# Last transposition of a head pair moved into the output sums' bank and ahead of the Newton product; the recurrence's results kept in one bank on diagonal quarters of the matrix unit

## The chip, the cores and the metric

The kernel runs on one core of one Trainium2 chip. A core has five engines that run their own instruction queues and wait for each other by semaphores: TensorE (PE in the profile, matrix products; its weight loads are PEld), VectorE (DVE), ScalarE (ACT), GpSimd (POOL) and SyncE (SP, which here issues the transfers). PE writes its results into PSUM, a small memory of eight banks of 2 KB a partition, and DVE and ACT read them from there; everything else on the core lies in SBUF.

The metric is the device time of one execution in microseconds (us). Before the change it is 1246.86 us, the median of three runs (1245.12, 1246.86 and 1247.34). A difference under 0.2% (about 2.5 us) is about what a measurement of this kernel can't tell from no change.

## The reference

Two layers over 256 positions of width 2048. Each layer normalises, makes one input projection, and feeds two groups of heads; their results are gated, joined, projected and added to the input. The part that the change touches is the group of 16 recurrent heads of width 64, each scanned in both directions (cut to what matters):

```python
for l in range(DEPTH):
    h = rms_norm(x, norm_g[l])
    proj = jnp.einsum('btd,dc->btc', h, w_in[l])
    ...
    y_rw = rwkv7_branch(r, k, v, xw, xa, w0[l], decay_up[l], a0[l], iclr_up[l], ...)
    ...
    y_at = window_attention(qh, kh, vh, sink[l]).astype(x.dtype)
    mix = jnp.concatenate([y_rw * jax.nn.silu(g_rw), y_at * jax.nn.silu(g_at)], axis=-1)
    x = x + jnp.einsum('btc,cd->btd', mix, w_out[l])

def wkv_scan(r, decay, k, v, kk, a, reverse):
    def step(S, inp):
        r_t, w_t, k_t, v_t, kk_t, a_t = inp
        s_kk = jnp.einsum('bhvk,bhk->bhv', S, kk_t)
        S = (S * w_t[:, :, None, :]
             - s_kk[..., None] * (a_t * kk_t)[:, :, None, :]
             + v_t[..., None] * k_t[:, :, None, :])
        return S, jnp.einsum('bhvk,bhk->bhv', S, r_t)
    ...

# in rwkv7_branch, behind both directions' scans:
mu = jnp.mean(y, -1, keepdims=True)
var = jnp.mean(jnp.square(y - mu), -1, keepdims=True)
yn = (y - mu) * lax.rsqrt(var + LNX_EPS)
yn = yn * lnx_g... + lnx_b...
out = yn + bonus * vh
```

## The kernel before

**Chunks and pairs.** The 256 positions are cut into four chunks of 64, and the heads are worked two at a time: eight pairs a layer, one head in partitions 0 to 63 and one in 64 to 127 (`half[0]`, `half[1]`). A product of 64x64 uses one quarter of PE's array, named by the half of the partitions it reads and the half it writes. Within a chunk the recurrence is a triangular system; its inverse is built by doubling blocks (levels of 2 up to 32) and by one Newton step.

**The work of one pair** is three generators, cut at `yield` into steps:
- `scan_p`: decays, keys and gates of the pair.
- `scan_i`: the masked products GE (L718 on PE, L724 on DVE, one of each for each direction), AB and AL, their fp16 parts (L733 on ACT, L764 on DVE), the transposes `pt` (L741, L749) that ACT reads as `bt` (L754) and, in four copies, as first values of the state `suv` (L759); then the inverse, level by level, from products `pq` and `pd` (L803 at the first level; L813, L819, L821 at the others) that DVE puts into two matrices `tv` and `tt` under masks (L806, L808, L809, L822, L823); last the Newton product `pf` (L829 to L834) and, in two steps of their own, FN (L836) and `pn` (L840), from which DVE makes `vf` in one operation over 128 partitions x 512 elements (L842).
- `scan_b`: the recurrence over the four chunks. For each: `pr` (L866), copied as `rh` (L869, at the first chunk two copies of L872), `pu` (L885), copied to the state `suv` (L890), the next state `pS` (L895, L897), and the output sums `py` (L877, L902). Behind the last chunk: the sums of squares (L913 to L915), the normalised output `ysq` (L917), its transposition on PE `pz` (L922), which ACT scales to `t` (L924), to which DVE adds `bv` (L925) and which `mix_split` gates and splits into MH and ML (L614 to L616), the operand of the output projection.

**PSUM.** `ps_main` holds two banks of the projections' sums `pm`. `ps_c` holds one bank `pcc` (the states of a pair) and one bank `py` (the output sums, in its first half; the second half holds one `pr` of the first chunk). `ps_w` holds two buffers of two banks, which all the other products (pza, pk, pbn, pg, pt, pq, pd, pf, pn, pu, pyt and the attention's) take in turn, in the order in which the program asks for them: each waits for the readers of the product that had the buffer two requests earlier. `wpair` takes such a buffer, `wbank` takes one and uses its first half.

**Windows and slots.** The big projections run beside these steps. Their weights are converted in tiles of 128x512 into a high part on ACT (L215, `hi`) and a low part on DVE (L216, `lo`), and a step of a projection is three products over 256 columns (L273, L274, L275). A window has 14 slots (numbered 0 to 13); in each slot the program first issues the scans' steps, then four or five projection steps, 64 in a window. Window w works on four pairs at once: the last step of pair w-4's `scan_b`, the two last steps of pair w-3's `scan_i` (`pf` in slot 0, `pn` in slot 1) and its `scan_b` (a step in each slot from 1 to 13), pair w-2's `scan_i` up to its last level (slots 0 to 13), and pair w-1's `scan_p`. The tables `STAGE_P`, `STAGE_I`, `STAGE_B` say in which slots. The last step of pair w-4 (`pz` and what follows) stands in slot 3. Each layer has four windows that are alike, with all four pairs at work (called steady below; 42.8 us each). The one ahead of them, called the first window below, has no pair w-4 yet; thinner ones stand ahead of it, and behind the steady ones come windows in which the attention's operations take the place of `scan_p`. Of these the tenth of a layer (382 to 425 us in the first layer, called the late window below) still has `scan_i`, `scan_b` and the last step of a pair in it.

PE's order is the program's order; the order of ACT and DVE is made by a scheduler that places instructions by priority, with that of `scan_b` raised by 95 (`PRIO_B`).

Of the kernel before, what the change touches and what calls it, by code (L numbers as in the profile page):

```python
# [9 lines left out]
F32 = mybir.dt.float32  # L10
# [5 lines left out]
AF = mybir.ActivationFunctionType  # L16
ALU = mybir.AluOpType
# [4 lines left out]
T = 256  # L22
# [13 lines left out]
P_NG, P_MU0, P_MU1, P_KK, P_KA, P_RK, P_LG, P_LB, P_A0 = 0, 16, 42, 68, 76, 84, 92, 100, 108  # L36
# [7 lines left out]
SLOTS = 14  # L44
STAGE_P = [4, 6, 7, 8, 9, 10, 11, 13]
STAGE_I = (list(range(SLOTS)), [0, 1])
STAGE_B = (list(range(1, 14)), [3])
ATT = [
    [4, 11],
    [1, 3, 6, 8, 11, 13],  # L50
# [78 lines left out]
def hybrid_trunk_kernel(ctx, tc, xT, wi, wv, wo, par, fing, dup, iup, sink, pos, cst, out):  # L129
    nc = tc.nc  # L130
    V, A, G, PE, SY = nc.vector, nc.scalar, nc.gpsimd, nc.tensor, nc.sync

    def pool(name, bufs, **kw):
        return ctx.enter_context(tc.tile_pool(name=name, bufs=bufs, **kw))
# [471 lines left out]
    def layer(l):  # L606
        L = layers[l]
        prm = lambda o, j: PR[:, l, o + j : o + j + 1]
# [99 lines left out]
        def scan_i(p, t):  # L708
            VV, BK, MV = t["v"], t["BK"], t["MV"]
            flat = lambda x: x.rearrange("p d c j -> p (d c) j")  # L710
            GE = st("ge", [2, 2, NC, 2, 64], bufs=2)
            GE = [GE[:, h] for h in range(2)]
            GEd = lambda d: pick(GE[0], every, d * NC * 128, [2 * NC * 128, 2], [128, NC], [1, 128])
            for d in range(2):
                pg = wpair("pg")
                for c in range(NC):
                    for h in range(2):
# [4 lines left out]
                            start=True, stop=True,  # L722
# [32 lines left out]
            SUV = st("suv", [2, NC, 2, 64], bufs=2)  # L755
# [26 lines left out]
            TT = st("tt", [2, NC, 64], F16)  # L782
# [43 lines left out]
            o = lambda d, c, h: pf[half[h ^ d], d, c * 64 : (c + 1) * 64]  # L826
# [11 lines left out]
            pn = wbank("pn")  # L838
            for d, c, h in dch:
                PE.matmul(pn[half[h ^ d], d * T + c * 64 : d * T + (c + 1) * 64], hx(FN, d, c, h), hx(TT, d, c, h), start=True, stop=True)  # L840
            VF = st("vf", [2, NC * 64])
            V.scalar_tensor_tensor(  # L842
                VF.rearrange("p d x -> p (d x)"), TT.rearrange("p d c j -> p (d c j)"), 2.0, pn, op0=ALU.mult, op1=ALU.add
            )
            t["VF"] = VF
            yield

        def scan_b(p, t):
            GE, MV, BT, SUV, PC, bv = (t[n] for n in ("GE", "MV", "BT", "SUV", "PC", "bv"))


            pc = ps_c.tile([128, 512], F32, tag="c", name="pcc")
            pS = pc[:, 0:128].rearrange("p (d j) -> p d j", d=2)
            pyt = ps_c.tile([128, 512], F32, tag="y", name="py")
            py = pyt[:, 0:256].rearrange("p (c j) -> p c j", j=64)
            for i in range(NC):
                ci = [order[d][i] for d in range(2)]

                here = lambda h, i=i: pick(SUV, half[h], i * 128 + h * 64, [NC * 128 + (NC - 1 - 2 * i) * 128, 2], [1, 64])

                pr = [pc[:, 128:192], pc[:, 192:256] if i else pyt[:, 256:320]]
                for d in range(2):
                    for h in range(2):

                        r = half[1 - h] if i == 0 else every
                        PE.matmul(pr[d][half[h ^ d]], GE[h][r, d, ci[d], 0, :], SUV[r, d, ci[d], h, :], start=True, stop=True)  # L866
                RH = st("rh", [2, 64], bufs=2)
                if i:
                    A.activation(RH, pc[:, 128:256].rearrange("p (d j) -> p d j", d=2), AF.Copy)  # L869
                else:  # L870
                    for d in range(2):
                        A.activation(RH[:, d, :], pr[d], AF.Copy)  # L872
                yield
                if i > 0:
                    for d in range(2):
                        for h in range(2):
                            PE.matmul(  # L877
                                py[half[h], ci[d], :], MV[half[h], d, ci[d], 1, :], SUV[half[h], d, ci[d], h, :],
                                start=False, stop=False, skip_group_check=True,
                            )  # L880
                pu = wpair("pu")
                for d in range(2):
                    for h in range(2):
                        x = half[h ^ d]
                        PE.matmul(pu[half[h], d, 0:64], t["VF"][x, d, cs(ci[d])], RH[x, d, :], start=True, stop=True)  # L885
                if 0 < i < NC - 1:
                    for h in range(2):
                        PE.matmul(pS[half[h]], ident[half[h], half[h]], here(h), start=True, stop=False, skip_group_check=True)  # L888
                for h in range(2):
                    A.activation(here(h), pu[half[h], :, 0:64], AF.Copy)  # L890
                yield
                if i < NC - 1:
                    for d in range(2):
                        for h in range(2):
                            PE.matmul(pS[half[h], d, :], BT[:, h, d, i, :], SUV[:, d, ci[d], h, :], start=(i == 0), stop=True, skip_group_check=True)  # L895
                    for h in range(2):
                        V.tensor_tensor(  # L897
                            here(h, i + 1), pS[half[h]], pick(PC, half[h], i, [2 * NC - 1 - 2 * i, 2], [0, 64]), op=ALU.mult
                        )
                for d in range(2):  # L900
                    for h in range(2):
                        PE.matmul(  # L902
                            py[half[h], ci[d], :], GE[h][:, d, ci[d], 1, :], SUV[:, d, ci[d], h, :],
                            start=(i == 0 and d == 0), stop=(i >= NC // 2), skip_group_check=True,
                        )
                if i < NC - 1:
                    yield


            ysq = st("ysq", [NC, 64])  # L910
            yv = st("yv", [NC])
            for c in range(NC):
                A.activation(ysq[:, c], py[:, c], AF.Square, accum_out=yv[:, c : c + 1])  # L913
            V.tensor_scalar(yv, yv, 1.0 / 64, LNX_EPS, op0=ALU.mult, op1=ALU.add)
            G.tensor_tensor(yv, yv, mhalf, op=ALU.pow)  # L915
            yield
            V.tensor_tensor(ysq, py, yv.unsqueeze(2).to_broadcast([128, NC, 64]), op=ALU.mult)  # L917
            yield
            pz = wbank("pyt")
            for c in range(NC):  # L920
                for h in range(2):
                    PE.matmul(pz[half[h], cs(c)], ysq[half[h], c, :], ident[half[h], half[h]], start=True, stop=True)  # L922
            Zt = st("t1", [T], bufs=3)
            A.activation(Zt, pz[:, 0:T], AF.Identity, scale=prm(P_LG, p), bias=prm(P_LB, p))  # L924
            V.tensor_tensor(Zt, Zt, bv, op=ALU.add)  # L925
            mix_split(p, Zt, t["gr"])
            yield
# [3 lines left out]
        def scans(w):  # L931

            gens = []
            for lag, scan, at in ((4, scan_b, STAGE_B[1]), (3, scan_i, STAGE_I[1]), (3, scan_b, STAGE_B[0]), (2, scan_i, STAGE_I[0]), (1, scan_p, STAGE_P)):
                p = w - lag
                if 0 <= p < NP:
                    if (scan, p) not in chains:
                        chains[scan, p] = scan(p, L.ts[p])
                    gens.append((chains[scan, p], at))
            return gens  # L940
# [119 lines left out]
    for a, b in ((0, 2), (2, 4), (4, 8), (8, 12), (12, 16)):  # L1060
        x = X2[:, a:b, :]
# [83 lines left out]
```

## Time and profile before

| | before |
|---|---|
| device time, median of 3 runs | 1246.86 us |
| device time of the profiled execution | 1247.3 us |
| span of the profiled execution | 1245.5 us |
| mean granted TensorE clock | 0.987 |
| busy share of the span: PE, DVE, ACT, POOL | 95%, 75%, 59%, 2% |
| chain that ended last: PE, DVE, issue, ACT, DMA | 48%, 18%, 16%, 11%, 4% |
| of that chain on L273, L274 and L275 (the projections' products) | 13%, 11%, 11% |

The span runs from the first to the last instruction; the device time is 1.8 us longer. Busy shares are averages over the span, and the chain is followed back from the last instruction to what released each one. In the timeline a row gives the start, the time to the end of the last of the group, the engine, the line, the operation, the tile written and the tiles read, the shape and the count, and in brackets how long the engine stood idle before it and who released it. A product of fp32 numbers counts as two matrix instructions in these rows. The ends of matrix products are modelled, so differences of starts are the better measure on PE.

### The profile page before, as it was taken

The page shows a single profiled execution, that of the slowest core. Times are in us where ns is not written, and L with a number is a line of the kernel's source. Part 1 is how long each engine was busy: PE and PEld are TensorE (multiplying, and loading weights), DVE is VectorE, ACT ScalarE, POOL GpSimd, SP SyncE. Part 2 cuts the span into 40 slices and gives each one's busy share as a digit, 9 for nine tenths or more (in the row PEclk, how much of TensorE's full clock was granted, in tenths as well). Part 3 has the DMA queues.
Part 4 walks back from the last instruction along what each step waited for, and adds up shares of the span by engine and source line. Part 5 has one row for each costly group of instructions (what it writes and reads, how often), then busy time and mean ns, then how long its engine had stood idle before and what let it go on. Part 6 is the DMA issues. An engine that isn't in the chain of part 4 may idle for free.

```text
span 1245.5 us, 38032 instructions
## 1 busy us (share of the span) xinstructions
PE 1184.3 (95%) x16140; PEld 1092.3 (88%) x16140; DVE 937.5 (75%) x2082; ACT 739.9 (59%) x1838; POOL 19.0 (2%) x23
## 2 busy tenths in 40 slices
PE   6989999999998999999999999999999989999996
PEld 6978888888887989989998888888888888899996
DVE  6878878887976678856666888878887766786654
ACT  6646665766565466645555656665766555675553
POOL 0000000000000000000000000000000000000000
PEclk9999999999999999999999999999999999999998
DMA  7443233322322434466554433233223324435653
GB/s 246 156 143 122 88 116 109 105 93 94 134 77 93 133 109 142 140 204 224 210 182 143 143 110 119 93 111 109 104 93 100 112 99 131 140 130 174 212 190 119
DMA packets 60410, 166.70 MB, mean 134 GB/s; under 512 B 7728, under 2 KB 22736, under 8 KB 60240
## 3 DMA queue, kind: packets, MB, share of 16 engines
q1 hardware_dynamic: 60240, 164.27, 38.5%
q8 instruction: 126, 2.06, 0.7%
q14 instruction: 44, 0.36, 0.1%
HBM read 157.43 MB, written 4.19 MB: 130 GB/s over the span
## 4 chain that ended last, share of the span: by engine, by line
PE 48%; DVE 18%; issue 16%; ACT 11%; DMA 4%; SPq 1%; POOL 0%; DVEq 0%; POOLq 0%; ACTq 0%
PE pm L273 13%; PE pm L275 11%; PE pm L274 11%; DVE lo L216 3%; DMA g<-dup 3%; PE pg L718 2%; DVE kd L665 2%; ACT hi L215 2%; DVE ge L724 2%; ACT AB L733 2%; ACT suv L759 2%; DVE lw L659 2%; ACT ge L771 1%; DMA rrot<-u 1%; ACT bt L754 1%
## 5 line engine op out<-in xcount | busy, mean ns | idle before, releaser
L273 PE MATMUL pm<-XH,hi 128*128 128x256 f32 x1664 | 498.1, 299 | 14.5 <-ACT XH L178 6.1
L275 PE MATMUL pm<-XH,lo 128*128 128x256 f32 x1664 | 471.4, 283 | 11.2 <-DVE lo L216 11.2
L274 PE MATMUL pm<-XL,hi 128*128 128x256 f32 x1664 | 470.6, 283 | 0.1
L215 ACT ACTIVATE hi<-raw 128x512 fp32r<-128x512 f32 x560 | 329.6, 625 | 212.1 <-PE pm L274 170.0
L216 DVE TENSOR_TENSOR lo<-raw,hi 128x512 fp32r<-128x512 f32 x560 | 369.0, 687 | 84.0 <-ACT hi L215 76.7
L273 PEld LDWEIGHTS pm<-XH,hi 128*128 128x128 f32 x1664 | 316.5, 190 | 40.2 <-issue 13.0
L275 PEld LDWEIGHTS pm<-XH,lo 128*128 128x128 f32 x1664 | 316.8, 190 | 14.6 <-DVE lo L216 14.4
L274 PEld LDWEIGHTS pm<-XL,hi 128*128 128x128 f32 x1664 | 317.3, 191 | 0.8 <-DVE XL L179 0.8
L273 PE MATMUL pm<-MH,hi 128*128 128x256 f32 x512 | 145.5, 284 | 2.3 <-ACT hi L215 2.3
L275 PE MATMUL pm<-MH,lo 128*128 128x256 f32 x512 | 145.2, 284 | 0.1
L274 PE MATMUL pm<-ML,hi 128*128 128x256 f32 x512 | 145.0, 283 | 0.0
L273 PEld LDWEIGHTS pm<-MH,hi 128*128 128x128 f32 x512 | 97.9, 191 | 3.2 <-ACT hi L215 2.5
L275 PEld LDWEIGHTS pm<-MH,lo 128*128 128x128 f32 x512 | 97.8, 191 | 0.4 <-DVE lo L216 0.4
L274 PEld LDWEIGHTS pm<-ML,hi 128*128 128x128 f32 x512 | 98.0, 191 | 0.0
L890 ACT ACTIVATE suv<-pu 64x128 f32<-64x128 f32 x128 | 34.5, 270 | 24.8 <-PE pcc L888 13.6
L724 DVE TENSOR_TENSOR ge<-pg,C 128x1024 f32<-128x1024 f32 x32 | 39.1, 1221 | 3.5 <-PE pg L718 3.5
L970 ACT ACTIVATE mv<-mv,mx 128x257 f32<-128x257 f32 x64 | 31.9, 504 | 15.9 <-DVE mx L967 15.9
L733 ACT ACTIVATE AB<-ge 64x512 f16<-64x512 f32 x32 | 20.2, 630 | 34.3 <-DVE ge L724 33.9
L718 PE MATMUL pg<-mv,bk 64*128 64x128 f32 x512 | 37.2, 285 | 0.0
L822 DVE CAST_PREDICATED tv<-LV,pd 128x256 f16<-128x256 uint8 x80 | 34.0, 426 | 4.1 <-PE pd L821 3.7
L815 ACT ACTIVATE QF<-pq 128x256 f16<-128x256 f32 x80 | 30.8, 385 | 6.8 <-PE pq L813 5.5
L823 DVE CAST_PREDICATED tt<-LV,pd 128x256 f16<-128x256 uint8 x80 | 34.0, 425 | 0.0
(241 smaller groups left out, 1833.7 us busy)
## 6 DMA issues: line engine op xcount, KB each, us to landing
raw<-wi SPq DMA_DIRECT2D x207, 512.0 KB, 3.8
raw<-wo SPq DMA_DIRECT2D x64, 512.0 KB, 3.8
raw<-wv SPq DMA_DIRECT2D x8, 512.0 KB, 3.6
rrot<-u SPq DMA_DIRECT2D x80, 32.0 KB, 2.3
vg<-xT SPq DMA_DIRECT2D x16, 128.0 KB, 3.6
xd<-vg SPq DMA_DIRECT2D x16, 128.0 KB, 3.6
vg<-xd SPq DMA_DIRECT2D x16, 128.0 KB, 3.5
g<-dup SPq DMA_DIRECT2D x16, 97.0 KB
```

The source lines that it names most:

```text
L215: A.activation(hi[:, q], raw[:, q], AF.Copy)
L216: V.tensor_tensor(lo[:, q], raw[:, q], hi[:, q].bitcast(F32), op=ALU.subtract)
L273: PE.matmul(pm, wh, rh[:, kk, :], start=(kk == 0), stop=False)
L274: PE.matmul(pm, wh, rl[:, kk, :], start=False, stop=False)
L275: PE.matmul(pm, wl, rh[:, kk, :], start=False, stop=(kk == 15))
L718: PE.matmul(pg[:, h, c * 128 : (c + 1) * 128], BK[half[h], d, c, 1 - h : 3 - h, :].rearrange("p s j -> p (s j)"), MV[half[h], d, c].rearra ...
L724: V.tensor_tensor(GEd(d), pg.rearrange("p h (c x) -> p h c x", c=NC), gm[d].unsqueeze(1).unsqueeze(1).to_broadcast([128, 2, NC, 128]), op= ...
L733: A.activation(flat(AB[half[h]]), GE[h][half[h]].rearrange("p d c s j -> p (d c) s j")[:, :, 0, :], AF.Copy)
L822: V.copy_predicated(t_sub(TC), t_mask, flat4(pd[:, :, 0:128]))
L823: V.copy_predicated(v_sub(TT), v_mask, flat4(pd[:, 0, 128:384].rearrange("p (d x) -> p d x", d=2)))
L890: A.activation(here(h), pu[half[h], :, 0:64], AF.Copy)
L970: A.activation(Sc[:, h, q, 0:257], Sc[:, h, q, 0:257], AF.Exp, scale=0.125, bias=mx[:, q : q + 1], accum_out=den[:, q : q + 1])
```

## The change

It has three parts.

First, `pz` no longer takes a buffer of `ps_w`: it is written into the second half of the pair's own bank of output sums (`pyt[:, T : 2 * T]`), which the first chunk's `pr` no longer uses. And its step is issued in slot 1 instead of slot 3 (`STAGE_B`), where it stands ahead of pair w-3's `pn`. With it move the ACT copy to `t`, the DVE addition of `bv`, and the three operations of `mix_split`. No transfer belongs to that step.

Second, `pr`, `pu` and `pS` of a chunk lie in one tile of the bank of states, asked for anew for each chunk, `pc` of [128, 3, 2, 64]. So `pu` takes no buffer of `ps_w` either. `pr` of the first chunk and `pu` are computed with each head reading and writing its own half of the partitions (two quarters of PE's array, on the diagonal) where before the second direction crossed over (four quarters). `rh` of the first chunk is one ACT copy and not two.

Third, for that the second direction of `vf` must lie in the other half of the partitions, so `vf` is written by three DVE operations (one of 128 partitions x 256, two of 64 partitions x 256 that cross over) in place of one of 128 x 512.

```diff
-STAGE_B = (list(range(1, 14)), [3])
+STAGE_B = (list(range(1, 14)), [1])
...
             VF = st("vf", [2, NC * 64])
-            V.scalar_tensor_tensor(
-                VF.rearrange("p d x -> p (d x)"), TT.rearrange("p d c j -> p (d c j)"), 2.0, pn, op0=ALU.mult, op1=ALU.add
-            )
+            for o, i, d in ((every, every, 0), (half[0], half[1], 1), (half[1], half[0], 1)):
+                V.scalar_tensor_tensor(
+                    VF[o, d], TT[i, d].rearrange("p c j -> p (c j)"), 2.0, pn[i, d * T : (d + 1) * T], op0=ALU.mult, op1=ALU.add
+                )
...
-            pc = ps_c.tile([128, 512], F32, tag="c", name="pcc")
-            pS = pc[:, 0:128].rearrange("p (d j) -> p d j", d=2)
...
-                pr = [pc[:, 128:192], pc[:, 192:256] if i else pyt[:, 256:320]]
+                pc = ps_c.tile([128, 3, 2, 64], F32, tag="c", name="pcc")
+                pS = pc[:, 2]
...
-                        PE.matmul(pr[d][half[h ^ d]], GE[h][r, d, ci[d], 0, :], SUV[r, d, ci[d], h, :], start=True, stop=True)
+                        PE.matmul(pc[half[h], 0, d, :], GE[h][r, d, ci[d], 0, :], SUV[r, d, ci[d], h, :], start=True, stop=True)
                 RH = st("rh", [2, 64], bufs=2)
-                if i:
-                    A.activation(RH, pc[:, 128:256].rearrange("p (d j) -> p d j", d=2), AF.Copy)
-                else:
-                    for d in range(2):
-                        A.activation(RH[:, d, :], pr[d], AF.Copy)
+                A.activation(RH, pc[:, 0], AF.Copy)
...
-                pu = wpair("pu")
                 for d in range(2):
                     for h in range(2):
-                        x = half[h ^ d]
-                        PE.matmul(pu[half[h], d, 0:64], t["VF"][x, d, cs(ci[d])], RH[x, d, :], start=True, stop=True)
+                        PE.matmul(pc[half[h], 1, d, :], t["VF"][half[h], d, cs(ci[d])], RH[half[h], d, :], start=True, stop=True)
...
-            pz = wbank("pyt")
+            pz = pyt[:, T : 2 * T]
```

What moves, at three places of a steady window. The first is PE's order in slot 1 (pn is the Newton product's second half, q and tt its operands; L915 is the changed kernel's line of pz):

```order
 L274 MATMUL pm<-XL,hi 128x256
 L275 MATMUL pm<-XH,lo 128x256
+L915 MATMUL py<-C,ysq 64x64 x8
 L840 LDWEIGHTS q_2653
 L840 MATMUL pn<-tt,q_2653 64x64
```

And in slot 3 of the same window (L895 and L902 are the next state and the output sums before, L888 and L895 the same two in the changed kernel):

```order
 L274 MATMUL pm<-XL,hi 128x256
 L275 MATMUL pm<-XH,lo 128x256
-L922 MATMUL pyt<-C,ysq 64x64 x8
-L895 MATMUL pcc<-suv,bt 64x64 x4
-L902 MATMUL py<-suv,ge 64x64 x4
+L888 MATMUL pcc<-suv,bt 64x64 x4
+L895 MATMUL py<-suv,ge 64x64 x4
 L803 LDWEIGHTS AB
 L803 MATMUL pq<-tv,AB 64x32
```

The eight transposing products go from slot 3, where they stood between the projection and L803, to slot 1 ahead of pn.

The second place is DVE's order in slots 1 and 2, first before the change (ge is GE, tv and tt the inverse's two matrices, set to the unit matrix by L784):

```order
L784 COPY tv<-EYE 128x512
L724 TENSOR_TENSOR ge<-pg,C 128x2x512
L842 SCALAR_TENSOR_TENSOR vf<-tt,pn 128x512
L784 COPY tt<-EYE 128x512
L724 TENSOR_TENSOR ge<-pg,C 128x2x512
L764 TENSOR_TENSOR AL<-ge,AB 64x512 x2
```

and behind the change (L843 is vf, L918 the addition of bv):

```order
L784 COPY tv<-EYE 128x512
L724 TENSOR_TENSOR ge<-pg,C 128x2x512
L843 SCALAR_TENSOR_TENSOR vf<-tt,pn 128x256
L918 TENSOR_TENSOR t_5355<-t_5355,bv 128x256
L843 SCALAR_TENSOR_TENSOR vf<-tt,pn 64x256
L614 SCALAR_TENSOR_TENSOR mf<-t_5355,vg 128x256
L843 SCALAR_TENSOR_TENSOR vf<-tt,pn 64x256
L784 COPY tt<-EYE 128x512
L616 TENSOR_TENSOR ML<-mf,MH 128x256
L724 TENSOR_TENSOR ge<-pg,C 128x2x512
```

Between the two operations that make GE there stood one operation of vf and the setting of tt; now there stand three of vf, the setting, and the three operations that follow pz.

The third place is DVE's order in slots 4 to 6, before (kr, iu and du belong to the projection's results, lw and mv to scan_p, L822 and L823 put pd into tv and tt):

```order
L402 SCALAR_TENSOR_TENSOR kr<-u,PR,kr 128x255
L442 TENSOR_TENSOR iu<-g,iuh 96x256
L656 TENSOR_SCALAR lw<-lw 128x512
L442 TENSOR_TENSOR du<-g,duh 97x256
L659 SCALAR_TENSOR_TENSOR lw<-MSK,lw 128x256 x2
L822 COPY_PREDICATED tv<-LV,pd 128x2x64x2
L823 COPY_PREDICATED tt<-LV,pd 128x2x64x2
L673 SCALAR_TENSOR_TENSOR mv<-pp,kkr 128x4x63
L674 SCALAR_TENSOR_TENSOR mv<-pp,kkr 128x4x63
```

and behind the change:

```order
L442 TENSOR_TENSOR du<-g,duh 97x256
L442 TENSOR_TENSOR iu<-g,iuh 96x256
L656 TENSOR_SCALAR lw<-lw 128x512
L659 SCALAR_TENSOR_TENSOR lw<-MSK,lw 128x256 x2
L673 SCALAR_TENSOR_TENSOR mv<-pp,kkr 128x4x63
L674 SCALAR_TENSOR_TENSOR mv<-pp,kkr 128x4x63
L822 COPY_PREDICATED tv<-LV,pd 128x2x64x2
L823 COPY_PREDICATED tt<-LV,pd 128x2x64x2
```

L673 and L674 now stand ahead of L822 and L823. This second order is the one that the first window of each layer has already before the change. The orders of SP and POOL are the same in both kernels, and requests for buffers of `ps_w` fall from 26 to 19 in a steady window.

More of the change, by code (lines that the diff above doesn't have):

```diff
@@ L889, in scan_b @@
                 for h in range(2):
-                    A.activation(here(h), pu[half[h], :, 0:64], AF.Copy)
+                    A.activation(here(h), pc[half[h], 1], AF.Copy)
                 yield
@@ L923, in scan_b @@
             Zt = st("t1", [T], bufs=3)
-            A.activation(Zt, pz[:, 0:T], AF.Identity, scale=prm(P_LG, p), bias=prm(P_LB, p))
+            A.activation(Zt, pz, AF.Identity, scale=prm(P_LG, p), bias=prm(P_LB, p))
             V.tensor_tensor(Zt, Zt, bv, op=ALU.add)
```

## The prediction

> **What bounds the kernel now.** I read the engines' shares first, then PE's waits by releaser, then the timelines of PE, DVE and ACT through one steady window, and the same through the first window.
>
> ```profile
> PE 1184.3 (95%) x16140; PEld 1092.3 (88%) x16140; DVE 937.5 (75%) x2082; ACT 739.9 (59%) x1838; POOL 19.0 (2%) x23
> ```
>
> The page's row of busy times: PE is almost always at work, so PE's own instructions and its short waits make the time.
>
> ```profile
> PE pq L803 <- ACT suv L759: 11.6, 12, 1.5
> ```
>
> In the view of waits (sum in us, count, longest) this is the wait that the change can take away: the first level's product pq, in slot 3, takes the buffer that ACT's fourth `suv` copy out of `pt` has yet to release. PE in a steady window, from slot 1 to slot 9:
>
> ```profile
> 298.58 0.34 PE L840 MATMUL pn<-tt,q 64*64 64x64 f16 x10
> ...
> 302.14 0.34 PE L885 MATMUL pu<-rh,vf 64*64 64x64 f32 x8
> 302.31 0.41 PE L741 MATMUL pt<-C,vg 64*64 64x64 f32 x16
> ...
> 304.79 0.68 PE L922 MATMUL pyt<-C,ysq 64*64 64x64 f32 x16
> 305.40 0.45 PE L895 MATMUL pcc<-suv,bt 128*64 128x64 f32 x8
> 305.68 0.40 PE L902 MATMUL py<-suv,ge 128*64 128x64 f32 x8
> 306.94 0.33 PE L803 MATMUL pq<-tv,AB 64*64 64x32 f16 x11 [0.86 <-ACT suv L759]
> ...
> 324.90 0.45 PE L895 MATMUL pcc<-suv,bt 128*64 128x64 f32 x8
> ```
>
> From slot 1's start at 298.58 to slot 9's at 324.90 are 26.32 us. pz takes 305.40 - 304.79 = 0.61, and from it to L803 are 306.94 - 304.79 = 2.15. The first window has no pz and no such wait:
>
> ```profile
> 133.39 0.45 PE L895 MATMUL pcc<-suv,bt 128*64 128x64 f32 x8
> 133.68 0.40 PE L902 MATMUL py<-suv,ge 128*64 128x64 f32 x8
> 134.01 0.33 PE L803 MATMUL pq<-tv,AB 64*64 64x32 f16 x10
> ...
> 136.37 0.45 PE L866 MATMUL pcc<-suv,ge 128*64 128x64 f32 x8
> ...
> 150.55 0.30 PE L813 MATMUL pq<-tv,AB 64*64 64x32 f16 x16 [0.26 <-DVE tt L823]
> ...
> 153.21 0.39 PE L275 MATMUL pm<-XH,lo 128*128 128x256 f32 x1 [0.48 <-DVE lo L216]
> 153.52 0.45 PE L895 MATMUL pcc<-suv,bt 128*64 128x64 f32 x8
> ```
>
> Here slot 3 is shorter by 2.15 - (134.01 - 133.39) = 1.53. Yet PE gives it back: it waits for DVE at slot 8's pq (0.26) and for a weight tile's low part (0.48), both outside the steady windows' waits. So behind a PE that is nearly full stands a second chain of almost the same length: AB on ACT, ACT's queue, the weight tiles, DVE's queue, and from there back to PE. Its start in the two windows:
>
> ```profile
> 130.16 1.28 ACT L733 ACTIVATE AB<-ge 64x512 f16<-64x512 f32 x2 [2.10 <-DVE ge L724]
> ```
>
> ```profile
> 301.56 1.28 ACT L733 ACTIVATE AB<-ge 64x512 f16<-64x512 f32 x2 [2.10 <-DVE ge L724]
> ```
>
> From AB to slot 9 are 153.52 - 130.16 = 23.36 in the first window and 324.90 - 301.56 = 23.34 in the steady one. In the first it is this chain that PE waits for; in the second PE's own work fills the time. The change gives the steady windows the first window's order on DVE in slots 4 to 6 (L673 and L674 ahead of L822 and L823). I therefore sum the new chain, not PE's savings.
>
> **The change part by part.** DVE now, in the steady window's slots 1 and 2, and in the late window, where operations of 128x256 stand back to back:
>
> ```profile
> 299.06 0.69 DVE L842 SCALAR_TENSOR_TENSOR vf<-tt,pn 128x512 f32<-128x512 f16 x1
> 299.79 0.29 DVE L784 COPY tt<-EYE 128x512 f16<-128x512 f16 x1
> 300.30 1.23 DVE L724 TENSOR_TENSOR ge<-pg,C 128x1024 f32<-128x1024 f32 x1 [0.22 <-PE pg L718]
> ```
>
> ```profile
> 389.36 0.43 DVE L495 TENSOR_TENSOR u<-u,TW 128x256 f32<-128x256 f32 x1 [1.97 <-DMA rrot<-u]
> 389.70 0.42 DVE L496 TENSOR_TENSOR rrot<-rrot,XA 128x256 f32<-128x256 f32 x1
> 390.04 0.29 DVE L784 COPY tt<-EYE 128x512 f16<-128x512 f16 x1
> 390.24 0.42 DVE L497 TENSOR_TENSOR u<-u,rrot 128x256 f32<-128x256 f32 x1
> ```
>
> A 128x256 operation costs 389.70 - 389.36 = 0.34 from start to start, the setting of tt 390.24 - 390.04 = 0.20. The trace has no vf of 64x256; I take 0.34 for it too, since the row beside it has as many elements a partition (bounds 0.20 and 0.43 by the rows above).
>
> *AB's start, counted from slot 1's start.* pz on PE ahead of pn: 0.61. From pn to vf: 299.06 - 298.58 = 0.48. Then vf, the addition of bv, vf, mf, vf: four at 0.34 and a last at 0.42 with 0.04 behind it as at 299.79 (299.06 + 0.69 + 0.04), 1.82. Setting tt: 0.20. ML: 0.34. From GE to AB: 301.56 - 300.30 = 1.26. Sum 4.71; now it is 301.56 - 298.58 = 2.98. So AB starts 1.73 later. Queued behind the addition of bv on DVE, which waits for ACT's `t`, are two parts of vf, tt, ML and GE, and for GE waits AB. `t` should be done in time: ACT is idle ahead of AB (2.10 in the row above), pz ends 0.68 behind slot 1's start, and the addition comes at 0.61 + 0.48 + 0.34 = 1.43.
>
> *From AB to slot 9.* The first window's 23.36, less what no longer stands ahead of the masks in slot 6:
>
> ```profile
> 136.74 0.69 DVE L216 TENSOR_TENSOR lo<-raw,hi 128x512 fp32r<-128x512 f32 x1 [1.58 <-ACT hi L215]
> 137.34 0.42 DVE L399 TENSOR_TENSOR u<-pm,rb 128x256 f32<-128x256 f32 x1
> 137.68 1.28 DVE L216 TENSOR_TENSOR lo<-raw,hi 128x512 fp32r<-128x512 f32 x2
> ```
>
> In the first window three low parts and L399 follow one another behind ACT's release; in the changed kernel's order L399 stands ahead of the first of two. One low part (137.34 - 136.74 = 0.60) and L399 (137.68 - 137.34 = 0.34) fall out: 22.42. Slot 1 to slot 9 is then 4.71 + 22.42 = 27.13, against 26.32: **+0.81**.
>
> *PE's own edits.* pz is moved, not shortened (0.61 leaves slot 3, 0.61 comes to slot 1). The wait of 0.86 at L803 goes, since its buffer is now one that was free long before; what is late next is the chain above, which swallows this and pz's 0.61. pu on two quarters instead of four: eight instructions take 302.31 - 302.14 = 0.17 now; pz, sixteen on two quarters, takes 0.61, so eight take 0.305, +0.13 for each of four chunks. Three of them stand in slots 2, 5 and 8 in the chain's shadow, the fourth behind slot 9: **+0.13**. [...]
>
> ACT's part costs nothing on the path: one `rh` less, and `t`, MH and the others now fall into its idle 2.10 ahead of AB. SP and POOL keep their order and no transfer moves. A bank asked for per chunk adds no wait that binds: pr already waits for both `suv` operations that read the state's bank.
>
> Per steady window +0.81 + 0.13 = +0.94; eight of them: **+7.5**.
>
> *The late window.* PE there:
>
> ```profile
> 391.85 0.46 PE L741 MATMUL pt<-C,vg 64*64 64x64 f32 x16 [1.72 <-DVE ge L724]
> ...
> 397.21 0.33 PE L803 MATMUL pq<-tv,AB 64*64 64x32 f16 x11 [1.54 <-ACT suv L759]
> ...
> 400.67 0.70 PE L866 MATMUL pcc<-suv,ge 128*64 128x64 f32 x8
> ```
>
> pt waits for DVE here, which itself waited for a transfer until 389.36. In the changed order nine operations follow from there (the rotation's four, bv, mf, ML and two of vf) and a last vf of 0.42 before pu can end: 389.36 + 9 x 0.34 + 0.42 = 392.84, with 0.06 of pu behind it 392.90, so pt is 1.05 later. pz (0.61) falls into that wait; the wait of 1.54 goes; three pu add 0.39. The slot behind L803 takes 400.67 - 397.21 = 3.46 against 136.37 - 134.01 = 2.36 in the first window: PE's products run slower behind a wait. I count these 1.10 as gained once, in the first layer. Together 1.05 - 0.61 - 1.54 + 0.39 = -0.71 in each layer and -1.10 once: **-2.5**. For the remaining windows, of which each has only some of the parts, I take 0, with 1.5 to either side.
>
> The sum is +7.5 - 2.5 = +5.0: the span 1245.5 becomes 1250.5 and the profiled run 1247.3 becomes 1252.3. That run lies 0.44 above the median of 1246.86; against the median the forecast is **1251.9**.
>
> **The rivals.**
>
> *Faster: the chain doesn't bind, PE's own work does.* Each steady window then gains 1.53 at slot 3, pays 0.61 in slot 1 and four times 0.13: -0.39, eight times -3.1, with the late windows' -2.5 in all -5.6: 1241.3. It decides if the chain from AB to slot 9 is shorter by 1.2 us (0.81 + 0.39) than I have it. For it: PE is busy 95% and the 11.6 us are real. Against it: the first window, with the same gain, takes no less. 0.25.
>
> *Near no change.* The chain is 0.6 shorter than summed (a vf of 64x256 at 0.20 instead of 0.34 would give 0.3 of it), or the wait at L803 only changes its cause, from `suv` to AB. The second ends near 4.71 + 1.28 = 6.0 behind slot 1's start, and L803 is due at 306.94 - 298.58 - 0.86 = 7.5, so this needs 1.5 of delay. +0.3 a window cancels the late windows: about 1247. 0.20.
>
> *Slower still: DVE starts each operation only when the last has ended.* Six operations at 0.42 instead of 0.34 put AB 0.5 later; eight windows +4: 1255.9. The same comes of `t` or MH arriving 0.5 late on ACT. Against it: the rows from 389.36 overlap. [...] 0.10.
>
> **How the numbers follow.** The forecast has 0.45, the rivals 0.25, 0.20 and 0.10. A measurement can't tell less than 0.2% (2.5 us) from no change: faster means under 1244.4, slower over 1249.4. Faster 0.25, same 0.20, slower 0.55. The range must take in the faster rival and the dearer chain, with the other windows' 1.5: 1240 to 1257. The forecast alone would be 1249 to 1255.
>
> **What would show it.** Right: in steady windows AB starts 4.7 behind slot 1's start, L803 has no wait for L759, pz takes 0.61 in slot 1, and new waits for DVE (L823, lo) stand between slots 4 and 8; the windows grow from 42.8 to 43.7. Wrong: AB starts by 4.1 or earlier, PE shows no new waits, and windows of 42.5. A wait of pu for vf in slot 2 of a steady window would be a mechanism that I haven't priced.

## The result, and the profile after

The changed kernel is slower: 1257.24 us as the median of four runs (1255.48 to 1258.58) against 1245.99 us before (four runs in the same comparison), a ratio of 1.0092 with a 95% interval of 1.0070 to 1.0114. A second comparison (below) gave 1255.27 against 1244.29 us, 1.0081 (1.0067 to 1.0095). The forecast was 1251.9: the right side, and under half of the size. The profiled run took 1255.48 us, the fastest of its four.

The row of busy times on the changed kernel's page:

```profile
PE 1188.7 (95%) x16140; PEld 1096.8 (87%) x16140; DVE 947.4 (76%) x2114; ACT 739.4 (59%) x1822; POOL 19.0 (2%) x23
```

PE is as full as before, with 4.4 us more of busy time. Its waits in the changed kernel (sum in us, count, longest):

```profile
PE pm L275 <- DVE lo L216: 19.8, 24, 1.6
...
PE pcc L888 <- ACT suv L883: 3.2, 10, 0.3
PE pq L813 <- DVE tv L822: 2.9, 6, 0.9
...
PE pcc L878 <- ACT MH L615: 1.9, 2, 1.1
PE pcc L865 <- DVE suv L890: 1.8, 3, 0.9
...
PE pcc L878 <- DVE vf L843: 1.4, 2, 0.7
```

The 11.6 us at L803 are gone, as meant. (By the program a steady window asks `ps_w` for 24 buffers before the change and 19 behind it, four `pu` and one `pz` fewer.) In their place PE waits longer for the low parts of weight tiles (19.8), for the state's copies, and in two windows for `vf` (L878 is `pu` here, L888 the next state, L865 `pr`). Before the change the waits for the low parts were:

```profile
PE pm L275 <- DVE lo L216: 11.2, 15, 1.6
```

PE in a steady window, from the window's start to the next one's (L915 is `pz`):

```profile
298.10 0.30 PE L829 MATMUL pf<-tv,NEYE 64*64 64x256 f16 x4
...
301.32 0.68 PE L915 MATMUL py<-C,ysq 64*64 64x64 f32 x16
301.84 0.32 PE L840 MATMUL pn<-tt,q 64*64 64x64 f16 x10
...
308.16 0.45 PE L888 MATMUL pcc<-suv,bt 128*64 128x64 f32 x8
...
308.77 0.33 PE L803 MATMUL pq<-tv,AB 64*64 64x32 f16 x10
...
318.38 0.45 PE L888 MATMUL pcc<-suv,bt 128*64 128x64 f32 x8 [0.34 <-ACT suv L883]
...
328.20 0.38 PE L275 MATMUL pm<-XH,lo 128*128 128x256 f32 x1 [0.83 <-DVE lo L216]
328.51 0.45 PE L888 MATMUL pcc<-suv,bt 128*64 128x64 f32 x8
...
341.90 0.30 PE L829 MATMUL pf<-tv,NEYE 64*64 64x256 f16 x4
```

L803 waits for nothing. The waits stand later: 0.34 in slot 6, 0.83 in slot 8. Slot 1 to slot 9 takes 328.51 - 301.32 = 27.19 us (26.32 before, 27.13 forecast), the window 341.90 - 298.10 = 43.80 (42.83 before, from one `pf` to the next). The changed kernel's DVE timeline in slots 1 and 2 (L918 adds `bv`):

```profile
302.30 0.42 DVE L843 SCALAR_TENSOR_TENSOR vf<-tt,pn 128x256 f32<-128x256 f16 x1 [0.59 <-PE pn L840]
302.65 0.43 DVE L918 TENSOR_TENSOR t<-t,bv 128x256 f32<-128x256 f32 x1
303.11 0.42 DVE L843 SCALAR_TENSOR_TENSOR vf<-tt,pn 64x256 f32<-64x256 f16 x1
303.56 0.43 DVE L614 SCALAR_TENSOR_TENSOR mf<-t,vg 128x256 f32<-128x256 f32 x1
304.02 0.42 DVE L843 SCALAR_TENSOR_TENSOR vf<-tt,pn 64x256 f32<-64x256 f16 x1
304.47 0.29 DVE L784 COPY tt<-EYE 128x512 f16<-128x512 f16 x1
304.68 0.42 DVE L616 TENSOR_TENSOR ML<-mf,MH 128x256 fp32r<-128x256 f32 x1
305.01 1.22 DVE L724 TENSOR_TENSOR ge<-pg,C 128x1024 f32<-128x1024 f32 x1
```

Eight operations stand there where four stood, and GE's second mask starts at 305.01, 3.69 behind slot 1's start. ACT's timeline behind it (L883 is the copy of `pu`):

```profile
306.27 0.63 ACT L733 ACTIVATE AB<-ge 64x512 f16<-64x512 f32 x1 [0.55 <-DVE ge L724]
306.81 0.54 ACT L883 ACTIVATE suv<-pcc 64x128 f32<-64x128 f32 x2
307.37 0.63 ACT L733 ACTIVATE AB<-ge 64x512 f16<-64x512 f32 x1
```

AB starts 306.27 - 301.32 = 4.95 us behind slot 1's start (2.98 before, 4.71 forecast). In the changed kernel's late window PE's timeline shows two stops at `pu`:

```profile
394.57 0.33 PE L878 MATMUL pcc<-rh,vf 64*64 64x64 f32 x4 [0.76 <-ACT MH L615]
395.58 0.71 PE L878 MATMUL pcc<-rh,vf 64*64 64x64 f32 x3 [0.68 <-DVE vf L843]
```

On DVE's timeline there, `vf` stands behind the rotation's multiplication, which waits for its transfer, and behind what follows:

```profile
392.32 0.42 DVE L495 TENSOR_TENSOR u<-u,TW 128x256 f32<-128x256 f32 x1 [2.48 <-DMA rrot<-u]
392.67 0.42 DVE L496 TENSOR_TENSOR rrot<-rrot,XA 128x256 f32<-128x256 f32 x1
393.00 0.42 DVE L918 TENSOR_TENSOR t<-t,bv 128x256 f32<-128x256 f32 x1
393.34 0.42 DVE L497 TENSOR_TENSOR u<-u,rrot 128x256 f32<-128x256 f32 x1
393.67 0.42 DVE L614 SCALAR_TENSOR_TENSOR mf<-t,vg 128x256 f32<-128x256 f32 x1
394.01 0.42 DVE L843 SCALAR_TENSOR_TENSOR vf<-tt,pn 128x256 f32<-128x256 f16 x1
```

(The profile names MH as the first stop's releaser; `pu` reads `rh` and `vf`, and `vf`'s first part ended at 394.43.) Behind the stops the granted clock falls. In this view of stretches of time the columns are the sum, busy times of PE, PEld, DVE, ACT and POOL, the granted clock, the DMA share and GB/s:

```profile
394.50:396.10 1.60, 0.73 (x10) 0.48 (x13) 1.52 (x5) 1.08 (x3) 0.00 (x0) 1.00 0.00 0
396.10:399.80 3.70, 3.70 (x42) 3.34 (x42) 3.67 (x6) 3.01 (x7) 0.00 (x0) 0.64 0.10 14
```

### The profile page after: what moved, and what is told of

It is laid out like the page before. It is cut to its first block, busy times and chain, and to the rows that moved or that the text cites. A ratio compares the mean times of both kernels' runs of the same rounds, so it can differ in the third digit from the quotient of the medians.

```text
span 1253.7 us, 38094 instructions
## 1 busy us (share of the span) xinstructions
PE 1188.7 (95%) x16140; PEld 1096.8 (87%) x16140; DVE 947.4 (76%) x2114; ACT 739.4 (59%) x1822; POOL 19.0 (2%) x23
## 5 line engine op out<-in xcount | busy, mean ns | idle before, releaser
L883 ACT ACTIVATE suv<-pcc 64x128 f32<-64x128 f32 x128 | 34.2, 267 | 19.9 <-PE pq L813 10.7
L822 DVE CAST_PREDICATED tv<-LV,pd 128x256 f16<-128x256 uint8 x80 | 34.2, 427 | 4.4 <-PE pd L821 3.9
L867 ACT ACTIVATE rh<-pcc 128x128 f32<-128x128 f32 x64 | 17.4, 271 | 31.3 <-PE pcc L865 30.9
L823 DVE CAST_PREDICATED tt<-LV,pd 128x256 f16<-128x256 uint8 x80 | 34.1, 426 | 0.0
```

Source lines behind the costliest of these rows:

```text
L822: V.copy_predicated(t_sub(TC), t_mask, flat4(pd[:, :, 0:128]))
L823: V.copy_predicated(v_sub(TT), v_mask, flat4(pd[:, 0, 128:384].rearrange("p (d x) -> p d x", d=2)))
L883: A.activation(here(h), pc[half[h], 1], AF.Copy)
```

## The experiments

The theory: DVE's operations that now stand ahead of GE's second mask (the tail of `pz`, that is the addition of `bv` and what follows it, and two more parts of `vf`) make AB late, and everything that hangs on AB reaches PE late; in the late windows they make `pu` wait behind a transfer. The rival: PE's own edits (two quarters, one bank) cost the time. Line numbers shift by a few in the edited kernels. Windows are read as above, from one `pf` to the next.

**tail_behind**: the changed kernel, the tail's operations behind `t` put back (`L.tt0` is the first level's last mask).

```diff
-STAGE_B = (list(range(1, 14)), [1])
+STAGE_B = (list(range(1, 14)), [1, 4])
...
-                    V.copy_predicated(one(TT, T), v_mask[:, 1], one(pq[:, 1], 0))
+                    L.tt0 = V.copy_predicated(one(TT, T), v_mask[:, 1], one(pq[:, 1], 0))
...
             A.activation(Zt, pz, AF.Identity, scale=prm(P_LG, p), bias=prm(P_LB, p))
-            V.tensor_tensor(Zt, Zt, bv, op=ALU.add)
+            yield
+            with tc.issue_after(L.tt0.ins) if L.tt0 is not None else ExitStack():
+                V.tensor_tensor(Zt, Zt, bv, op=ALU.add)
             mix_split(p, Zt, t["gr"])
```

> The changed kernel with one thing moved: pz and its copy to t stay in slot 1, but the addition of bv and what follows (mf, MH, ML) are queued on DVE behind L809, the last mask of the first level, as before the change; vf in three parts, the bank and the diagonal quarters stay. Theory (the time is lost because the tail's three DVE operations and vf's two more parts stand ahead of GE's second mask and make AB late, so that PE waits in slots 5 to 8): AB starts 3.6 us behind slot 1's start instead of 4.95, steady windows fall from 43.80 to 42.5 to 43.3, the kernel to 1246 to 1252. Rival (PE's own cost: two quarters instead of four, one bank for pr, pu and pS): AB is earlier but the windows stay at 43.6 to 43.8, the kernel at 1255 to 1257.

1247.82 us (12 runs) against 1246.56, ratio 1.0014 (1.0001 to 1.0028). Steady windows take 42.59, less than before the change, and PE waits for nothing in them:

```profile
294.90 0.30 PE L830 MATMUL pf<-tv,NEYE 64*64 64x256 f16 x4
...
337.48 0.30 PE L830 MATMUL pf<-tv,NEYE 64*64 64x256 f16 x4
```

AB starts 3.79 behind slot 1's start, a little later than the 3.6 expected. Of the 0.97 that a steady window lost the three operations' place explains all, and 0.24 more come back. The rival falls as the cause of the loss: the bank and the quarters are still in this kernel. But PE's own edits are not free. In these windows PE is busy for 42.43 us, before the change for 41.82 of 42.83: 0.6 more work, hidden because nearly all of PE's idle time went. In early_tail (below), which has neither the bank nor the two quarters, it is 41.92. The kernel as a whole stays 1.3 us above the one before: in the first profiles its first windows are 0.36 longer each, and the two windows behind the steady ones 2.6 longer in all over both layers.

**early_only**: the kernel before with `STAGE_B`'s 3 made a 1.

> The kernel before with its last step alone moved from slot 3 to slot 1 (pz still takes a buffer of its own; vf one operation, pu on four quarters as before). Theory: L803's wait goes, but the tail's DVE operations stand ahead of GE's second mask, AB starts about 4.3 us behind slot 1's start, and steady windows are longer than before by 0.4 to 1.0: 1249 to 1254. Rival (quarters and bank cost it): no slower than before, 1240 to 1246.

1252.41 us (6 runs), 1.0056 (1.0038 to 1.0074); steady windows 43.39, AB 4.64 behind slot 1's start, 0.3 later than expected. Moving the step alone, with no edit to quarters, banks or `vf`, costs over half of the loss, with no wait at L803.

**pz_slot3**: the changed kernel with `pz` back in slot 3.

```diff
-STAGE_B = (list(range(1, 14)), [1])
+STAGE_B = (list(range(1, 14)), [3])
...
-            pz = pyt[:, T : 2 * T]
+            pz = wbank("pyt")[:, 0:T]
```

> The changed kernel with pz back in slot 3 and in a buffer of its own (the bank of states, the diagonal quarters and vf in three parts stay). Theory: AB starts 3.4 us behind slot 1's start, 0.4 later than before; L803 waits for the copies out of pt as before, 1.0 to 1.3 a time; four pu at 0.13 more each: steady windows 43.2 to 43.7, the kernel 1250 to 1254. Rival (only the moved step costs): 42.8 and 1246.

1253.71 us (6 runs), 1.0062 (1.0038 to 1.0086); steady windows 43.14, a little under the expected 43.2 to 43.7; AB at 3.30; L803 waits again, 14.7 us in 12 instances. The other two parts cost 0.31 a steady window without the move.

**early_tail**: early_only with the tail's DVE operations queued as in tail_behind.

> The kernel before with pz moved to slot 1 and the tail's DVE operations queued behind L809 as in tail_behind; nothing else. Theory: PE saves L803's wait, AB starts 3.5 us behind slot 1's start, 0.5 later than before; if the chain from AB is all that holds PE, windows are 42.4 to 43.0 and the kernel 1243 to 1248; it is the best of the four. Rival (quarters and bank cost it): as early_only, 1240 to 1246, with no difference between the two.

1249.80 us (12 runs), 1.0022 (1.0005 to 1.0038). Steady windows are 42.75, in the expected range, AB at 3.82, 0.3 later than expected. The total is 2 us above the expected range: the windows behind the steady ones are longer (46.34 and 45.33 in the first layer, 44.83 and 44.55 before). So it is not the best of the four, and the steady windows are not the whole account.

**vf3_only and fill**, one run each: the kernel before with `vf` in three parts in place, and the kernel before with nothing but three more operations on DVE (`d` is 1 at GE's second mask).

```diff
+            with tc.issue_after(L.vf.ins):
+                for _ in range(3):
+                    L.fil = V.scalar_tensor_tensor(VF[:, 0], TT[:, 0].rearrange("p c j -> p (c j)"), 2.0, pn[:, 0:T], op0=ALU.mult, op1=ALU.add)
...
+                with tc.issue_after(L.fil.ins) if d and L.fil is not None else ExitStack():
+                    V.tensor_tensor(
+                        GEd(d),
...
```

> The kernel before with vf written by three operations of the changed kernel's sizes, each in place (no half crosses over), and nothing else: pu stays on four quarters, pz in slot 3. Theory: GE's second mask and AB come 0.4 later, L803's wait is 1.1 to 1.3, steady windows 43.1 to 43.3, near the 43.14 of pz_slot3, so that the quarters cost next to nothing there. Rival (the quarters cost pz_slot3 its 0.3): 42.8 to 42.9 here.

> The kernel before with three more DVE operations of 128x256 (the first half of vf written again, the same values) queued between vf and GE's second mask; PE, the banks and the order of the steps are untouched. Theory: AB starts 0.8 us later (three at 0.34, less the setting of tt, which moves behind the mask), L803's wait grows from 0.86 to 1.6, steady windows go from 42.83 to 43.5 to 43.9: the changed kernel's length with none of its PE edits. Rival (DVE's delay is covered; PE's own edits cost the time): 42.8 to 43.0.

vf3_only: 1250.4 us against 1245.17, steady windows 43.14, as in pz_slot3, with about the same waits at L803 (1.2). So the quarters cost nothing there that shows, and `vf`'s parts cost the 0.31. fill: 1259.7 us against 1245.17, steady windows 43.77, the changed kernel's length, with none of its edits. In its timelines of PE and ACT (L831 is `pf`, L842 `pn`, L735 AB):

```profile
296.38 0.30 PE L831 MATMUL pf<-tv,NEYE 64*64 64x256 f16 x4
...
299.59 0.34 PE L842 MATMUL pn<-tt,q 64*64 64x64 f16 x10
...
303.37 0.61 ACT L735 ACTIVATE AB<-ge 64x512 f16<-64x512 f32 x1
...
340.15 0.30 PE L831 MATMUL pf<-tv,NEYE 64*64 64x256 f16 x4
```

AB starts 3.78 behind slot 1's start, as expected; the first level waits only 1.06 and not 1.6, since the second half of AB and the copies out of `pt` come in another order; the rest appears as a wait for a weight tile (0.5), as in the changed kernel. The steady windows side by side:

| kernel | pz in slot | AB behind slot 1's start, us | wait at L803, us | steady window, us | first window, us |
|---|---|---|---|---|---|
| before | 3 | 2.98 | 0.86 | 42.83 | 42.86 |
| vf3_only | 3 | 3.28 | 1.2 | 43.14 | 43.14 |
| pz_slot3 | 3 | 3.30 | 1.1 | 43.14 | 43.20 |
| fill | 3 | 3.78 | 1.06 | 43.77 | 42.57 |
| tail_behind | 1 | 3.79 | none | 42.59 | 43.22 |
| early_tail | 1 | 3.82 | none | 42.75 | 42.83 |
| early_only | 1 | 4.64 | none | 43.39 | 42.83 |
| after | 1 | 4.95 | none | 43.80 | 43.26 |

With `pz` in slot 3, AB 0.30 to 0.32 later makes the window 0.31 longer, and 0.80 later 0.94. With `pz` in slot 1, early_only against early_tail has AB 0.82 later and 0.64 more, the changed kernel against tail_behind 1.16 later and 1.21 more.

One entry speaks against a fixed price for a late AB. In fill's first window AB is as late as in its steady ones (3.79 behind slot 1's start), and yet that window is 0.29 shorter than before the change. From AB to slot 9 it takes 151.79 - 129.53 = 22.26 there, in the steady window 326.86 - 303.37 = 23.49. The three operations also change the order that the scheduler gives DVE and ACT behind them, and that order is not the same in the two windows. How much of the loss is AB's lateness itself and how much the order that comes with it, these runs don't separate.

The totals hold more than the steady windows. The late windows of these six kernels take 43.85 to 46.92, where those of the kernel before take 42.85 to 44.55, so a total alone is no test of the account for the steady windows.

**after_again and before_again**: the two kernels once more, for second profiles.

> The changed kernel itself, for a second profile and a closer ratio. Expected: steady windows at 43.80 again; 1256 to 1258 as the median; the late windows within 1 us of 44.7 and 45.9 if their loss belongs to the change, elsewhere if it is the transfers' timing.

> The kernel before itself, for a second profile: steady windows at 42.83, the late windows within 1 us of 44.55 and 43.27 if they belong to the kernel and not to the transfers' chance.

after_again: 1255.27 us (6 runs), just under the expected range. Steady windows 43.80 to 43.83 and 42.83 to 42.86: these repeat to 0.03. The late windows don't: 45.91 and 45.32 in the two layers (44.72 and 45.88 in the first profile) and, for the kernel before, 42.85 and 43.46 (44.55 and 43.27). The means are 45.46 and 43.53. So one of the two late windows lies outside the expected 1 us in each kernel: 1.2 in the changed one (45.91 against 44.72), 1.7 in the one before (42.85 against 44.55). Part of what varies is the clock. Behind L803's wait in the first layer's late window the kernel before had 0.64 in its first profile (stretches of time, columns as above):

```profile
397.20:400.60 3.40, 3.39 (x33) 3.18 (x32) 2.24 (x6) 2.90 (x7) 0.00 (x0) 0.64 0.00 0
```

and in its second 1.00:

```profile
395.20:397.60 2.40, 2.36 (x33) 2.17 (x32) 1.21 (x4) 2.24 (x4) 0.00 (x0) 1.00 0.00 0
```

**after_rope, tail_rope, before_rope**: the late windows. The rotation's operations are called ten projection steps later and queued behind GE's second mask, in the changed kernel, in tail_behind and in the kernel before (`L.ge2` is GE's mask).

```diff
-                V.tensor_tensor(raw, raw, CR, op=ALU.mult)
-                V.tensor_tensor(rot, rot, SR, op=ALU.mult)
+                def turn():
+                    with tc.issue_after(L.ge2.ins):
+                        V.tensor_tensor(raw, raw, CR, op=ALU.mult)
+                        V.tensor_tensor(rot, rot, SR, op=ALU.mult)
...
+                S.later(10, turn)
```

> The changed kernel with the rotation's six operations (L495 to L500) called ten projection steps behind their transfers, and its two multiplications queued on DVE behind GE's second mask, so that vf does not stand behind an operation that waits for a transfer. Theory for the late windows (pu stops twice because vf stands behind that operation, and PE's clock then falls to 0.57 to 0.64): the two stops at pu in the late windows (0.76 + 0.68 and 1.11 + 0.69) go, the clock stays at 1.00 there, each late window loses 1.5 to 3 us of its 44.7 and 45.9; steady windows stay at 43.80; the kernel comes to 1251 to 1254. Rival (the late windows differ by the transfers' chance timing alone): they stay within 1 us of 44.7 and 45.9, the kernel at 1256 to 1258.

> tail_behind and after_rope together. Theory: steady windows as in tail_behind (42.6), late windows 1.5 to 3 us shorter than its 43.9 and 45.0: the kernel at 1242 to 1246, below the kernel before by 1 to 4. Rival: as tail_behind, 1247 to 1249.

> The kernel before with the rotation's operations moved as in after_rope. It tells how much of after_rope's gain is the changed kernel's own loss. Theory: before the change the same transfer delays GE's second mask there (pt waits 1.72 and 1.28 for it), so this kernel gains as well, 1 to 3 us: 1243 to 1246. Rival (only the changed kernel loses there): no change, 1246 to 1247.

after_rope: 1249.60 us (6 runs), 1.0040 (1.0027 to 1.0054), 5.7 less than the changed kernel in the same comparison and a little better than expected. The late windows are 42.35 and 42.27; the steady ones stay at 43.80; neither stop at `pu` in slot 2 is left, and in the stretch from that slot on PE is busy throughout at a clock of 1.00:

```profile
394.90:398.60 3.70, 3.70 (x84) 3.31 (x82) 3.67 (x7) 3.09 (x8) 0.00 (x0) 1.00 0.04 14
```

before_rope: 1243.12 us (12 runs), 0.9980 (0.9968 to 0.9993): it gains 1.2, less than half; its late windows are 44.45 and 42.00. So of after_rope's 5.7 most is the changed kernel's own loss. tail_rope: 1240.94 us (12 runs), 0.9974 (0.9962 to 0.9986): faster than both kernels, and 1 us below the expected range. Its steady windows take 42.60, its late ones 40.90 and 42.96. With the tail's operations behind the first level's masks and the rotation behind GE, the change's bank, quarters and early `pz` remain. Of the 0.26% the moved rotation alone gives 0.20% (before_rope); the rest, 2.2 us between the two medians, is less than the 2.5 us that a measurement can tell, and the steady windows, 0.23 shorter each, are the better sign of it.

## Why the prediction was right in direction and wrong in size

**The steady windows were right in mechanism, and in sum closer than the terms deserved.** Forecast +0.94 each; measured 43.80 - 42.83 = 0.97. The mechanism is shown by tail_behind (take the late DVE operations away: 42.59) and by fill (add only such operations: 43.77). That the sum came out within 0.03 is luck in part, since errors of about 0.2 cancel in it. AB came at 4.95 and not 4.71: three of DVE's starts there lie 0.45 or 0.46 behind the neighbour's and not 0.34 (303.11, 303.56 and 304.02 above), and `pz` took 0.52 in slot 1 (301.84 - 301.32), not 0.61. From AB to slot 9 it took 328.51 - 306.27 = 22.24 and not 22.42. The prediction's reading that this stretch is a chain that holds PE in the first window is not confirmed by fill's first window, where AB is 0.81 later at no cost.

**The wait at L803 went and came back elsewhere**, as forecast: slots 6 and 8. One of the two causes that it named is there, the weight tile's `lo`; the other, the masks of L823, is not, and PE waits for ACT's copy of the state instead.

**The failed step is the late window, forecast at -2.5 for the two layers.** It measured 45.46 - 43.53 = +1.93 each, +3.9 in all, an error of 6.4 us, as much as the gap between the forecast +5.0 and the two measured +11.3 and +11.0. The prediction counted about rightly how long `pu` is held behind the transfer (3.48; the second stop ended 395.58 - 392.32 = 3.26 behind it). It failed in what it took from there. It counted L803's wait of 1.54 as gained and the slow stretch of 1.10 behind it as gone, and it ended the account at the slot behind L803. PE's busy time in the late windows shows both errors (two layers each, us):

| kernel | late windows | PE busy in them | mean granted clock |
|---|---|---|---|
| before, first profile | 44.55, 43.27 | 41.05, 39.61 | 0.96, 1.00 |
| before, second profile | 42.85, 43.46 | 39.66, 39.69 | 1.00, 1.00 |
| after, first profile | 44.72, 45.88 | 41.76, 41.72 | 0.96, 0.96 |
| after, second profile | 45.91, 45.32 | 41.82, 40.28 | 0.96, 1.00 |
| after_rope | 42.35, 42.27 | 39.95, 39.83 | 1.00, 1.00 |
| before_rope | 44.45, 42.00 | 40.95, 39.44 | 0.96, 1.00 |

Of the +1.93 a window 1.4 are longer busy time and 0.5 longer waiting. Waiting was forecast to fall by 1.10 (1.05 - 0.61 - 1.54). The two stops at `pu` and the later slots took that back: AB, in the first layer's late window 397.26 - 386.43 = 10.83 behind the window's start and before the change 391.83 - 383.01 = 8.82, was 2.0 late there as well, and PE waits 0.7 at L865 (for the state's copy) and 0.6 at L813 (for a mask) behind it.

Busy time was forecast at -0.16 (three `pu` at 0.13, less 1.10 once in two layers). But the slow stretch was not L803's alone, and the second profile of the kernel before has none in its late windows. It follows a stop of PE, and the change makes stops of its own, at `pu`: the clock fell to 0.64 behind them (0.57 in the second layer, 0.72 in after_again's first, 1.00 in its second), in three of four windows, where before the change it fell in one of four. The clock is not all of it: the window without a slow stretch takes 45.32 as well, since PE waits 5.04 in it. after_rope shows the two together: without the operation that waits ahead of `vf`, both stops are gone, the clock stays at 1.00, and the late windows take 42.3.

**The rest** I had taken as 0 with 1.5 to either side: the first windows cost 0.39 each (43.24 against 42.84, as means of two profiles), and vf3_only (43.14) shows `vf`'s parts in most of it; the window behind the steady ones gained 0.36 each (44.38 against 44.74 as means of two profiles). Together under 0.1. With the steady windows' 7.8 and the late windows' 3.9 this makes 11.7, against 11.0 to 11.3.

**The rivals.** "PE's own work decides" fell: it needed AB by 4.1 at the latest, and AB came at 4.95. Its arithmetic comes true once AB is early enough: tail_behind's 42.59 is 0.24 under before, where the rival had 0.39. "Slower still" named the right size (1255.9), and its mechanism held in part: three of the starts came only when the neighbour had ended, which cost 0.35 and not 0.5. But the steady windows were no longer for it than forecast; what brought the total there is the late windows. DVE's starts show both: operations that overlap start 0.34 apart, those beside a part of `vf` that crosses 0.45.

**Why the clock fell behind some stops and not behind others** shows in finer stretches of the changed kernel's first late window:

```profile
393.75:397.15 3.40, 1.83 (x38) 1.40 (x38) 3.33 (x9) 2.34 (x6) 0.00 (x0) 1.00 0.05 17
397.20:400.55 3.35, 3.35 (x26) 3.13 (x28) 3.02 (x8) 3.20 (x6) 0.00 (x0) 0.50 0.29 72
400.60:404.00 3.40, 3.40 (x67) 3.05 (x64) 1.88 (x6) 2.98 (x8) 0.00 (x0) 1.00 0.20 80
```

In the clock records of all 13 profiles a slow stretch at half clock lasts 3.41 us or twice that (the end of the run aside), and within a profile the slow stretches start whole multiples of 3.41 us apart. Cut on that grid, between 60 and 1220 us, every full-speed stretch in which PE was busy under 0.49 of the time was followed by a slow one (30 of 30), none in which it was busy over 0.59 (0 of 4186), and between the two 14 of 46. So it matters how a stop lies on the grid. L803's wait of 1.54 in the kernel before fell into one stretch in the first layer (busy 0.55, slow behind it) and was split over two in the second (0.75 and 0.80, not slow). What decides between 0.49 and 0.59 stays open.

## What to carry to other kernels

When work is moved earlier on one engine, look at what it drags along on the queues of the others: here eight small products moved by two slots took three vector operations with them, ahead of the one operation on which the next pair's whole chain hangs. A wait removed from an engine that is 95% busy pays only if the chain behind it has slack; the cheapest test is to delay that chain alone (three operations written twice) and see whether the loss appears, with an eye on whether the scheduler reorders what stands behind. And a window in which an engine's queue holds an operation that waits for a transfer has to be summed by itself to its end, with every operation that now stands behind the transfer.

## What the runs showed of the hardware

- DVE operations of 0.42 us follow one another in two ways here. In the changed kernel's late window (the timeline from 392.32 above) operations of 128x256 overlap, 0.33 to 0.35 us from start to start. fill's three, which write the same place, take 1.33 together, more than the 2 x 0.34 + 0.42 = 1.10 of three that overlap. In the changed kernel's steady window (from 302.30 above) each part of `vf` that crosses, and the operation behind it, begins only when the one ahead has ended, 0.45 or 0.46 from start to start. Three parts took 1.32 us where two halves crossed. DVE's timeline in pz_slot3:

```profile
300.92 1.32 DVE L843 SCALAR_TENSOR_TENSOR vf<-tt,pn 128x256 f32<-128x256 f16 x3
```

and 1.18, still more than 1.10, where none did, in vf3_only:

```profile
299.28 1.18 DVE L843 SCALAR_TENSOR_TENSOR vf<-tt,pn 128x256 f32<-128x256 f16 x3
```

- Behind the two stops of PE at `pu` (0.76 + 0.68 = 1.44 us) the changed kernel lost about as much again. From `pu` to the next state it takes 308.16 - 305.40 = 2.76 in a steady window, and 399.80 - 394.57 = 5.23 in the late one, of which the second stop is 0.68: 1.79 more. The slow stretches have a clock of 0.50, last 3.41 us or twice that and lie on a grid of their own, and the same kernel shows one in one profile and not in the next (0.64 and 1.00 behind L803's wait in the kernel before).
- The same clock goes with the spread between runs of one kernel. Among the 23 runs of the kernel before in tail_behind's comparison the shortest (1242.28 us) has a mean granted clock of 0.995 and the two longest (1249.65 and 1249.83) have 0.986 and 0.987; time and clock correlate at -0.71. It is part of the spread, not all of it.
